# The first norm's x loaded turned for seven of eight feature blocks, and a fourth output block in the opening

## The chip, the cores and the metric

The kernel runs on one core of a Trainium2 chip. The metric is the device time of one execution in microseconds (us), taken as the median of several runs. The engines are named as in the profile: PE (TensorE matmul; PEld its weight loads), DVE (VectorE), ACT (ScalarE), POOL (GpSimd) and SP (SyncE, which issues nearly all DMAs here).

## The reference

The reference is one decoder block in float32 on a sequence of 1024 tokens with 1024 features. Only its beginning is touched by the change:

```python
mod = silu(c) @ w_ada + b_ada                      # 6 x 1024 from the condition c
sh1, sc1, g1, sh2, sc2, g2 = split(mod, 6)
h = rms_norm(x, pre_norm1_w) * (1 + sc1) + sh1     # per token 1/rms, per feature scale and shift
proj = h @ w_in                                    # 1024 x 7696
z, xbc, dt_raw, q, k, v, gates = split(proj)       # gates: two x 1024 columns
...                                                # SSD branch, attention branch, merge, conv-FFN
```

So h = x * rstd[token] * a1[feature] + sh1[feature], with a1 = pre_norm1_w * (1 + sc1).

## The kernel before, in words

Activations are kept turned: features on the 128 partitions, tokens along the row. The 1024 features are eight blocks k = 0..7 (`KD`), the 1024 tokens two halves of 512. Products are in float32 by three passes: every operand is split into a high part (rounded, `hi`) and a rest (`lo`), and hi*hi + hi*lo + lo*hi is accumulated in PSUM, in this kernel 128x128 weights against 512 tokens each.

**The opening.** x lies in memory with tokens as rows. Eight tiles of 128 tokens are loaded (`load_x`), each squared and summed (`square_x` on ACT, `square_v` on DVE), `rstd_x` makes 1/rms (DVE, then a power on POOL), and `scale_x` multiplies each tile by it. For a unit (k, half), `turn_x` has PE transpose four 128x128 pieces into a PSUM bank (L209); `make_h` has ACT make from the bank the high part `hT[k][half]` and the full value `hr` (L215, L216), each as scale a1 and bias sh1; the function that it returns has DVE subtract for the low part (L217). `products(k, half)` then runs nine products on PE: for each of three output blocks (two of `w_xbc`, the first of `w_gate`) hi*hi, lo*hi, hi*lo (L241 to L243). Their weights come in three pieces of feature blocks (`load_first` 0-2, 2-4, 4-8), split by `first_high` (ACT) and `first_low` (DVE). The eight PSUM banks are: `px0` four (two blocks, two halves), `ps_wa` two (gate block 0, two halves), and `ps_wb` and `ps_wc` one each, which take the transposes in turn.

The modulation values of block k come from two 128x1024 tiles of `w_ada1` (shift and scale), loaded by `load_mod(k)` into a ring of eight; `mod_sum` multiplies each by a row silu(c) that is spread over the partitions and sums along the row (DVE, L200), and `mod_end` (DVE, L203, L204) makes sh1 and a1 of that block.

**Behind the opening** come gate blocks 1, 2 and 3: `gate_load`, `gate_split`, and for each half 24 products into a `ps_wa` bank (`gate_half`, L116 to L118), which `gate_out` (ACT, L396) turns into a tanh in `vev` and SP stores. Beside them DVE and ACT make the sums and differences of the quarters of h (`sub`, `hi_of`, `lo_of`, for the operands t2, t1, t3, t4) for what follows: eight passes m = 0..7, each a pair of output blocks computed by Strassen-like seven products (`x_mms(m, p)`, L462 to L464, 12 matmuls each), with the weights' sums (`x_sum`) and splits (`x_split`, `x_ahead` three products ahead) on DVE and ACT. Passes 1 to 3 also hold the remaining modulation sums (`ada_sum`).

The order of the work on PE, DVE, ACT and SP is written out by hand (`tc.manual_schedule`): each engine takes its instructions in the order of the program, and waits on semaphores. A DMA that SP issues has one of eight semaphores and waits until the DMA eight places ahead has landed. Large tiles lie in 43 slots of 4 KB a partition (`Slots`, `SL.get`, `SL.put`).

Of the kernel before, what the change touches and what calls it, by code (L numbers as in the profile page):

```python
# [17 lines left out]
P = 128  # L18
# [44 lines left out]
def kernel(ctx: ExitStack, tc: tile.TileContext, a: dict, out: bass.AP, dbg=None):  # L63
# [82 lines left out]
    A.activation(scl, cT, AF.Silu)  # L146


    hT = [[new_hl(f"hT{k}_{h}") for h in range(2)] for k in range(KD)]
# [3 lines left out]
    junk = SL.get("junk0")  # L153
# [9 lines left out]
    hr = [[[SL.get(f"hr{r}{h}{i}", F32, (P, 2, HALF)) for i in range(2)] for h in range(2)] for r in range(2)]  # L163
    sh1 = const("sh1", [P, KD])
    a1 = const("a1", [P, KD])
    b1c = const("b1c", [P, KD])
    msum = const("msum", [P, KD, 2])

    def load_x(i):
        SP.dma_start(xts[i], a["x"][i * P : (i + 1) * P, :])  # L170

# [19 lines left out]
    n_b = 0  # L191

    def next_bank(name):
        nonlocal n_b
        n_b += 1
        return (ps_wb, ps_wc)[n_b % 2](name)

# [4 lines left out]
    def mod_end(j):  # L202
        V.tensor_tensor(sh1[:, j : j + 1], msum[:, j, 0:1], vec[:, V_B1S + j : V_B1S + j + 1], op=ALU.add)  # L203
        V.scalar_tensor_tensor(a1[:, j : j + 1], msum[:, j, 1:2], b1c[:, j : j + 1], vec[:, V_PN1 + j : V_PN1 + j + 1], op0=ALU.add, op1=ALU.mult)  # L204

    def turn_x(k, half):
        ps = next_bank(f"xtr{k}_{half}")
        for q in range(4):
            T.transpose(ps[:, q * P : (q + 1) * P], xts[4 * half + q][:, k * P : (k + 1) * P], ident)  # L209
        return ps  # L210

    def make_h(k, half, ps):
        xh = hr[k // KH][half][k % KH // 2][:, k % 2, :]
        hi, lo = hT[k][half][:, 0, :], hT[k][half][:, 1, :]
        A.activation(hi, ps, AF.Identity, scale=a1[:, k : k + 1], bias=sh1[:, k : k + 1])  # L215
        A.activation(xh, ps, AF.Identity, scale=a1[:, k : k + 1], bias=sh1[:, k : k + 1])  # L216
# [4 lines left out]
    raw0 = [wp.tile([P, KD, P], F32, tag="wraw", name=f"wf{b}_raw", bufs=3) for b in range(3)]  # L221
    w0 = [[wp.tile([P, KD, P], F32R, tag=f"w{n}", name=f"wf{b}_{n}", bufs=4) for n in ("hi", "lo")] for b in range(3)]
    px0 = [ps_mm("xbc0"), ps_mm("xbc1")]
    pg0 = [ps_wa("gs0_0"), ps_wa("gs0_1")]

# [10 lines left out]
    def products(k, half):  # L236
        for b in range(3):
            o = px0[b][:, half, :] if b < 2 else pg0[half]
            wh, wl = w0[b][0][:, k, :], w0[b][1][:, k, :]
            xh_, xl_ = hT[k][half][:, 0, :], hT[k][half][:, 1, :]  # L240
            T.matmul(o, wh, xh_, start=(k == 0), stop=False)  # L241
            T.matmul(o, wl, xh_, start=False, stop=False)
            T.matmul(o, wh, xl_, start=False, stop=(k == KD - 1))  # L243

    EN = mybir.EngineType
    with tc.manual_schedule(engines={EN.PE, EN.DVE, EN.Activation, EN.SP}):
        for i in range(4):
            load_x(i)
        load_mod(0)
# [3 lines left out]
        load_mod(1)  # L253
        load_first(2, 4)
        load_mod(2)
        load_mod(3)
        load_first(4, 8)
        V.tensor_scalar(b1c, vec[:, V_B1C : V_B1C + KD], 1.0, None, op0=ALU.add)
        for h in range(2):
            pr = next_bank(f"srow{h}")  # L260
# [6 lines left out]
        square_x(3)  # L267
        rstd_x(2)
        scale_x(0, False)
# [5 lines left out]
        mod_end(0)  # L275
        load_mod(4)
        pt0 = turn_x(0, 0)
        for b in range(3):
            first_high(b, 0, 2)
        low = make_h(0, 0, pt0)  # L280
        first_low(0, 0, 2)
        low()
        first_low(1, 0, 2)
        first_low(2, 0, 2)
# [6 lines left out]
        rstd_x(6)  # L291
        scale_x(4, False)
# [3 lines left out]
        pt0 = turn_x(0, 1)  # L296
        mod_sum(1, 0)
        low = make_h(0, 1, pt0)
        mod_sum(1, 1)
        mod_end(1)  # L300
        load_mod(5)
        low()
        mod_sum(2, 0)
        units = [(k, h) for k in range(1, KD) for h in range(2)]
        last = (0, 1)
        for n, u in enumerate(units):
            pt0 = turn_x(*u)
            low = make_h(*u, pt0)
            j = u[0] + 1 + u[1]
            if j < KD:  # L310
                mod_sum(j, 1 - u[1])
                if u[1] == 0:
                    mod_end(j)
                    if j + 4 < KD:
                        load_mod(j + 4)
            low()
            if n in (0, 3):
                for b in range(3):
                    first_high(b, *((2, 4) if n == 0 else (4, 8)))
            if n == 1:  # L320
                for b in range(3):
                    first_low(b, 2, 4)
            elif 3 < n < 7:
                first_low(n - 4, 4, 8)
            products(*last)
            last = u
        products(*last)
        SL.put(junk, *adat, srow, prod, *xts)

# [201 lines left out]
    with tc.manual_schedule(engines={EN.PE, EN.DVE, EN.Activation, EN.SP}):  # L531
# [3 lines left out]
        for n in ("t2", "t1", "t3", "t4"):  # L535
            HX[n] = [new_hl(f"x{n}_{k}") for k in range(KH)]
# [1799 lines left out]
```

## Time and profile before

| what | value |
|---|---|
| median of 3 runs | 1851.14 us (1849.91 to 1851.85) |
| profiled execution | 1848.95 us, its span 1847.1 us |
| PE busy / DVE / ACT in the span | 99% / 70% / 48% |
| first product of the opening | 16.92 us |
| first product of the gate blocks | 65.54 us |
| first product of pass m=0 | 98.18 us |

The span is the time from the first to the last instruction; the profiled execution took 1.85 us more than its span. Times of single instructions are counted from the span's start. A row of the order of time gives start, duration, engine, line, operation, out<-in, and in brackets what the engine was idle for before it.

### The profile page before, as it was taken

What the parts mean: (1) busy time and instruction counts of PE and PEld (TensorE: products, weight loads), DVE (VectorE), ACT (ScalarE), POOL (GpSimd) and SP (SyncE); (2) the same over time, 40 slices, a digit from 0 to 9 for tenths busy, and PEclk for the clock granted to TensorE, in tenths of its full rate; (3) what the DMA queues carried; (4) which work ended last, traced back from release to release, by engine and by line L of the source; (5) the groups of instructions that cost most, each with busy time, mean ns of one, the idle gap of its engine ahead of it and who ended that gap; (6) DMA issues with size and microseconds to landing.
All of it is one profiled execution on the core that took longest, in us unless ns stands there. A gap on an engine that the chain in (4) does not pass through costs nothing.

```text
span 1847.1 us, 24410 instructions
## 1 busy us (share of the span) xinstructions
PE 1822.4 (99%) x8974; PEld 1527.3 (83%) x8974; DVE 1294.9 (70%) x1980; ACT 888.3 (48%) x1720; POOL 144.5 (8%) x128
## 2 busy tenths in 40 slices
PE   6999999999999999999999999999999999999998
PEld 4888899988888888888888888888888888888887
DVE  6777867799654257777667464487898888876545
ACT  6644543456532145565556232565545454455532
POOL 0000000266421000000000100000000000000001
PEclk9999999999999999999999999999999999999999
DMA  8365367687646856566734754122333222378744
GB/s 335 133 216 183 103 208 238 219 315 268 242 125 185 260 132 172 165 170 164 198 104 146 236 196 177 52 95 103 103 120 108 103 97 98 109 235 309 243 158 165
DMA packets 130217, 322.57 MB, mean 175 GB/s; under 512 B 14881, under 2 KB 38833, under 8 KB 130098
## 3 DMA queue, kind: packets, MB, share of 16 engines
q1 hardware_dynamic: 129138, 317.86, 52.3%
q0 software_dynamic: 960, 3.15, 0.5%
q8 instruction: 71, 1.16, 0.3%
q14 instruction: 48, 0.39, 0.1%
HBM read 225.79 MB, written 95.17 MB: 174 GB/s over the span
## 4 chain that ended last, share of the span: by engine, by line
PE 91%; DVE 4%; ACT 3%; issue 1%; DMA 1%; POOL 0%; SPq 0%; DVEq 0%; POOLq 0%; ACTq 0%
PE upx L1744 4%; PE upx L1743 4%; PE upx L1745 4%; PE o L1437 3%; PE dx L2108 2%; PE dx L2107 2%; PE dx L2106 2%; PE upy L1743 2%; PE upy L1744 2%; PE upy L1745 2%; PE v L950 2%; PE z L117 2%; PE z L118 2%; PE z L116 2%; PE dy L2108 2%; PE dy L2107 2%
## 5 line engine op out<-in xcount | busy, mean ns | idle before, releaser
L1743 PE MATMUL upx<-t,wu_t 128*128 128x512 f32 x264 | 103.2, 391 | 0.5 <-DVE cv L2171 0.4
L1744 PE MATMUL upx<-t,wu_t 128*128 128x512 f32 x264 | 102.9, 390 | 0.2 <-DVE t L1861 0.2
L1745 PE MATMUL upx<-t,wu_t 128*128 128x512 f32 x264 | 102.7, 389 | 0.0
L1717 ACT ACTIVATE wu_t<-sab 128x512 fp32r<-128x512 f32 x57 | 34.1, 627 | 128.3 <-DVE sab L1734 128.3
L1425 ACT COPY aT<-at 128x512 f32<-128x512 f32 (+2 forms) x96 | 46.0, 479 | 96.3 <-PE at L1424 96.3
L1437 PEld LDWEIGHTS o<-vt,aT 128*128 128x128 f32 x576 | 75.3, 191 | 9.2 <-ACT aT L1425 4.6
L95 DVE TENSOR_TENSOR g_lo<-gst,g_hi 128x1024 fp32r<-128x1024 f32 (+1 forms) x42 | 47.5, 1135 | 49.0 <-ACT g_hi L94 48.9
L1437 PE MATMUL o<-vt,aT 128*128 128x128 f32 x576 | 80.9, 276 | 0.4 <-ACT aT L1425 0.2
L94 ACT ACTIVATE g_hi<-gst 128x1024 fp32r<-128x1024 f32 (+1 forms) x42 | 41.4, 988 | 63.8 <-DMA gst<-gld_s 35.8
L1398 DVE TENSOR_REDUCE nmx<-sc 128x1 f32<-128x640 f32 (+3 forms) x64 | 65.6, 1025 | 2.2
L1378 PE MATMUL sc<-kst,qst 128*128 128x512 f32 (+2 forms) x192 | 63.8, 340 | 0.0
L1379 PE MATMUL sc<-klo,qst 128*128 128x512 f32 (+2 forms) x192 | 63.3, 346 | 0.0
L1761 DVE SCALAR_TENSOR_TENSOR ug<-cg,vec,ug 128x1023 f32<-128x1023 f32 (+1 forms) x44 | 56.3, 1280 | 6.1 <-ACT ug L1760 5.3
L1743 PEld LDWEIGHTS upx<-t,wu_t 128*128 128x128 f32 x264 | 49.5, 188 | 11.6 <-DVE cv L2171 1.3
L1744 PEld LDWEIGHTS upx<-t,wu_t 128*128 128x128 f32 x264 | 49.6, 188 | 10.6 <-DVE t L1861 0.5
L1745 PEld LDWEIGHTS upx<-t,wu_t 128*128 128x128 f32 x264 | 49.6, 188 | 10.4
L1721 DVE TENSOR_TENSOR wu_t<-sab,wu_t 128x512 fp32r<-128x512 f32 x57 | 39.3, 690 | 26.6 <-ACT wu_t L1717 26.6
L1761 DVE SCALAR_TENSOR_TENSOR uv<-cv,vec,uv 128x1023 f32<-128x1023 f32 (+1 forms) x44 | 56.2, 1278 | 0.9 <-ACT uv L1760 0.9
L1414 DVE RECIPROCAL rsm<-ssum 128x2 f32<-128x2 f32 x64 | 10.6, 166 | 62.4 <-ACT p L1411 35.1
L2227 POOL TENSOR_TENSOR rsf<-rsf,nhalf 128x1 f32<-128x1 f32 x8 | 5.2, 654 | 623.5 <-DVE rsf L2226 623.5
L1416 DVE SCALAR_TENSOR_TENSOR p<-p,coef,p 128x128 f32<-128x128 f32 (+3 forms) x64 | 52.4, 819 | 2.3
L2106 PE MATMUL dx<-wdt_hi,g_hi 128*128 128x512 f32 x132 | 51.3, 389 | 0.0
(537 smaller groups left out, 5923.4 us busy)
## 6 DMA issues: line engine op xcount, KB each, us to landing
adas<-in_w_ada SPq DMA_DIRECT2D x32, 512.0 KB, 5.1
wdr<-in_w_down SPq DMA_DIRECT2D x22, 512.0 KB, 6.2
wtd<-wds SPq DMA_DIRECT2D x22, 512.0 KB, 4.6
wuf<-in_w_up SPq DMA_DIRECT2D x22, 512.0 KB, 3.5
gld_s<-gsum SPq DMA_DIRECT2D x22, 512.0 KB, 2.8
gst<-gld_s SPq DMA_DIRECT2D x20, 512.0 KB, 4.9
wdt_raw<-wtd SPq DMA_DIRECT2D x20, 512.0 KB, 5.1
wuv<-in_w_up SPq DMA_DIRECT2D x19, 512.0 KB, 3.5
```

Source lines behind the costliest of these rows:

```text
L1378: T.matmul(sc[:, n0:n1], qs_[s][:, tsl], ks_[s][:, n0:n1], start=True, stop=False)
L1379: T.matmul(sc[:, n0:n1], qs_[s][:, tsl], kl[s][:, n0:n1], start=False, stop=True)
L1398: V.reduce_max(nmx[:, bq, s : s + 1], sc[:, :L], axis=AX.X, negate=True)
L1416: V.scalar_tensor_tensor(pr[0][:, :L], pr[1][:, :L], coef[:, bq : bq + 1], pr[0][:, :L], op0=ALU.mult, op1=ALU.add)
L1437: T.matmul(po_of[j, grp][:, qi, :], at[:, k, :], vt[j % 2][:, kt, :], start=(kt == 0), stop=(kt == i))
L1743: T.matmul(out_, wh, xh_, start=(k == 0 and first), stop=False, skip_group_check=not first)
L1744: T.matmul(out_, wh, xl_, start=False, stop=False, skip_group_check=not first)
L1745: T.matmul(out_, wl, xh_, start=False, stop=(k == end), skip_group_check=not first)
L1761: V.scalar_tensor_tensor(u[:, d:], c_[:, : S - d], fw[:, 2 - d : 3 - d], u[:, d:], op0=ALU.mult, op1=ALU.add)
L2106: T.matmul(o, gh[:, kk, tsl], wh, start=(k == 0 and not more), stop=False, skip_group_check=more)
L2107: T.matmul(o, gh[:, kk, tsl], wl, start=False, stop=False, skip_group_check=more)
L2108: T.matmul(o, gl[:, kk, tsl], wh, start=False, stop=(k == KF - 1), skip_group_check=more)
```

## The change

1. x is also given turned by the host (`xT`, features as rows). Only feature block 0 is still scaled and transposed on the chip. For k = 1..7 the tile `xT[k]` is loaded, and DVE multiplies it by a1 (per partition) and by a row of rstd that is spread over all partitions (`scale_t`); `make_h` reads that from SBUF and only adds sh1. The 56 other transposes fall away.
2. The row `xrow` is made in two halves: ACT scales the identity by rstd into four diagonal pieces (`diag_of`), one f32 matmul of ones against them (`row_of`) spreads the row, and ACT copies it from PSUM.
3. A fourth output block (the second of `w_gate`) joins the opening: 12 products for each unit, in the banks that the transposes had. It leaves the gate blocks, which are now 2 and 3.
4. `products` runs all blocks' hi*hi, then lo*hi, then hi*lo.
5. The modulation values of block 1 come from PE: 16 matmuls of one column (`mod_mm`), for which the host lays out these two tiles of `w_ada1` the other way. Those of blocks 2 to 7 end on ACT (`mod_end_act`).
6. x's first four tiles are issued right behind `crow`, ahead of the identity, `vec` and `cT`; silu of `cT` moves behind the first squares.
7. Gate block 2 is split ahead of time, with its high part used before its low part (`gate_half_late`); t4's sums, and the loads for `ada_sum`, move into pass m=0.

The diff, cut to its core:

```diff
     cT = const("cT", [P, KD])
-    SP.dma_start(cT, a["cT"])
     ident = const("ident", [P, P])
-    SP.dma_start(ident, a["ident"])
     vec = const("vec", [P, NVEC])
-    SP.dma_start(vec, a["vec"])
...
+    def load_xT(k):
+        SP.dma_start(xT[k].rearrange("p h t -> p (h t)"), a["xT"][k * P : (k + 1) * P, :])
...
+    def mod_mm(j, g, ps):
+        for k in range(KD):
+            T.matmul(ps[:, g : g + 1], adat[(2 * j + g) % NADA][:, k * P : (k + 1) * P], scl[:, k : k + 1], start=(k == 0), stop=(k == KD - 1))
...
+    def mod_end_act(j):
+        A.activation(a1[:, j : j + 1], msum[:, j, 1:2], AF.Identity, scale=vec[:, V_PN1 + j : V_PN1 + j + 1], bias=b1p[:, j : j + 1])
+        A.activation(sh1[:, j : j + 1], msum[:, j, 0:1], AF.Identity, bias=vec[:, V_B1S + j : V_B1S + j + 1])
...
+    def diag_of(half):
+        d = hr[0][1][1][:, half, :]
+        for q in range(4):
+            A.activation(d[:, q * P : (q + 1) * P], ident, AF.Copy, scale=rs1[:, 4 * half + q : 4 * half + q + 1])
+        return d
+
+    def row_of(half, ps):
+        T.matmul(ps, ones, hr[0][1][1][:, half, :], start=True, stop=True)
+
+    def scale_t(k, half):
+        t = xT[k][:, half, :]
+        V.scalar_tensor_tensor(t, t, a1[:, k : k + 1], xrow[:, half, :], op0=ALU.mult, op1=ALU.mult)
...
-    firsts = (("w_xbc", 0), ("w_xbc", 1), ("w_gate", 0))
+    firsts = (("w_xbc", 0), ("w_xbc", 1), ("w_gate", 0), ("w_gate", 1))
...
+    def products(k, half, bs=range(NF), kinds=(0, 1, 2)):
+        for kind in kinds:
+            for b in bs:
+                o = px0[b][:, half, :] if b < 2 else (pg0, pg1)[b - 2][half]
...
+                T.matmul(o, (wh, wl, wh)[kind], (xh_, xh_, xl_)[kind], start=(k == 0 and kind == 0), stop=(k == KD - 1 and kind == 2))
...
         for i in range(4):
             load_x(i)
+        SP.dma_start(ident, a["ident"])
+        SP.dma_start(vec, a["vec"])
+        SP.dma_start(cT, a["cT"])
         load_mod(0)
         load_first(0, 2)
         for i in range(4, 8):
             load_x(i)
         load_mod(1)
+        load_xT(1)
+        load_mod(2)
         load_first(2, 4)
-        load_mod(2)
+        load_xT(2)
         load_mod(3)
+        load_xT(3)
         load_first(4, 8)
...
+        diag_of(0)
+        mod_mm(1, 0, px0[0][:, 1, :])
+        row_of(0, px0[1][:, 1, :])
+        mod_mm(1, 1, px0[0][:, 1, :])
         scale_x(4, False)
         scale_x(5, True)
         scale_x(6, True)
         scale_x(7, False)
...
+        turn_x(1, pt1)
+        mod_end(1, px0[0][:, 1, 0:2])
...
+        A.copy(xrow[:, 0, :], px0[1][:, 1, :])
+        diag_of(1)
+        low01 = make_h(0, 1, pt1)
...
+        scale_t(1, 0)
+        mod_sum(2, 0)
+        products(0, 1, range(3), (0, 1))
...
+        row_of(1, pr)
+        A.copy(xrow[:, 1, :], pr)
+        low01()
+        products(0, 1, range(3), (2,))
+        pg1[1] = ps_wc("gs1_1")
+        products(0, 1, (3,))
...
+        for k in range(2, KD):
+            scale_t(k, 0)
+            scale_t(k, 1)
+            lows = []
+            for h in range(2):
+                lows.append(make_h(k, h))
+                if k == 3:
+                    first_high(2 * h, 4, 8)
+                    first_high(2 * h + 1, 4, 8)
...
+                if k == 4 and h == 0:
+                    for b in range(NF):
+                        first_low(b, 4, 8)
+                if k < KD - 1:
+                    mod_sum(k + 1, h)
...
+                lows[h]()
+                if h == 1 and k < KD - 1:
+                    mod_end_act(k + 1)
+                products(k, h)
...
+        gate_split(3)
         lo_of("t2", 3, r22)
-        pg = gate_half(1, 1)
+        for half in range(2):
+            gate_out(pg1[half], half, gsd[1])
...
         for k in range(KH):
             hi_of("t1", k, r12)
             sub(r11, r22, r11, k)
             lo_of("t1", k, r12)
-        gate_out(pg, 1, gsd[1])
+        pg2.append(gate_half(2, 1))
+        gate_out(pg2[0], 0, gsd[2])
...
+        pg3 = [gate_half(3, 0)]
+        gate_out(pg2[1], 1, gsd[2])
...
+                    if m == 0:
+                        for k in range(KH):
+                            sub(r21, r21, r22, k)
...
+                    if m == 0:
+                        for k in range(KH):
+                            hi_of("t4", k, r21)
...
+                    if m == 0:
+                        for k in range(KH):
+                            lo_of("t4", k, r21)
```

More of the change, by code (lines that the diff above doesn't have):

```diff
@@ L301 @@
+        low01 = make_h(0, 1, pt1)
         load_mod(5)
-        low()
+        load_xT(4)
+        scale_t(1, 0)
         mod_sum(2, 0)
[L304 to L326, printed above, removed]
@@ L327 @@
-        products(*last)
-        SL.put(junk, *adat, srow, prod, *xts)
+        products(0, 1, range(3), (0, 1))
+        pr = ps_wc("xrow1")
+        row_of(1, pr)
[4 more added lines that the diff above has]
+        products(0, 1, (3,))
+        low10 = make_h(1, 0)
+        mod_sum(2, 1)
+        load_mod(6)
+        load_xT(5)
+        scale_t(1, 1)
+        low10()
+        for b in range(NF):
+            first_high(b, 2, 4)
@@ L331 @@
+        gw[2] = w2
+        SL.put(srow, prod, raw3, xrow, *xT[1:])
     order = (("b11", "X"), ("b21", "Z"), ("t2", "X"), ("t1", "Y"), ("t3", "X"), ("b22", "Y"), ("t4", "X"))
```

190 lines of the change are left out of this document (104 added, 86 removed).

## The prediction

> **What bounds the kernel now.** I read the page's busy shares and chain first, then the opening in stretches, then engine by engine.
>
> ```profile
> PE 1822.4 (99%) x8974; PEld 1527.3 (83%) x8974; DVE 1294.9 (70%) x1980; ACT 888.3 (48%) x1720; POOL 144.5 (8%) x128
> ...
> PE 91%; DVE 4%; ACT 3%; issue 1%; DMA 1%; POOL 0%; SPq 0%; DVEq 0%; POOLq 0%; ACTq 0%
> ```
>
> TensorE (PE) is busy in 99% of the span and is 91% of the chain that ended last. So a change in the opening is worth what it does to one moment: when PE enters the Strassen pass m=0 (first `x_mms`), because behind that pass the instructions of every engine stand in the same order in both programs. The stretches (columns: PE, PEld, DVE, ACT, POOL busy, granted clock, DMA share, GB/s):
>
> ```profile
> 15.00:20.00 5.00, 3.18 (x8) 1.90 (x7) 3.76 (x10) 3.89 (x7) 0.00 (x0) 1.00 1.03 419
> 20.00:25.00 5.00, 2.56 (x9) 1.58 (x9) 4.38 (x11) 2.38 (x4) 2.44 (x2) 0.90 1.04 394
> 25.00:30.00 5.00, 4.81 (x13) 3.11 (x12) 4.76 (x12) 3.73 (x7) 0.00 (x0) 0.50 1.04 403
> 35.00:40.00 5.00, 5.00 (x27) 4.04 (x26) 4.67 (x12) 3.94 (x8) 0.00 (x0) 1.00 1.02 402
> 40.00:45.00 5.00, 5.00 (x27) 4.16 (x26) 4.36 (x7) 3.20 (x5) 0.00 (x0) 1.00 0.46 155
> ```
>
> PE waits until about 25 us and is full from 30 us on; DMA is full until 40 us at about 400 GB/s and then eases. PE's own marks, from its order of time:
>
> ```profile
> 16.92 0.80 PE L241 MATMUL xbc<-hT,wf_hi 128*128 128x512 f32 x1 [1.64 <-ACT hT L215]
> ...
> 25.88 0.80 PE L241 MATMUL xbc<-hT,wf_hi 128*128 128x512 f32 x1
> ...
> 33.13 0.60 PE L209 MATMUL xtr<-ident,xt 128*128 128x128 f32 x4
> 33.48 0.47 PE L241 MATMUL xbc<-hT,wf_hi 128*128 128x512 f32 x1
> ...
> 35.99 0.48 PE L241 MATMUL xbc<-hT,wf_hi 128*128 128x512 f32 x1
> ...
> 65.54 0.39 PE L116 MATMUL gs<-hT,wgs_hi 128*128 128x512 f32 x1
> ...
> 98.18 0.39 PE L462 MATMUL xx<-hT,xw_b 128*128 128x512 f32 x1
> ```
>
> At 35.99 the products of feature block k=2 begin, at 65.54 the gate blocks, at 98.18 pass m=0. A unit (one k, one half of the tokens) lasts 35.99 - 33.48 = 2.51 us. The gate blocks are 6 halves of 24 products: (98.18 - 65.54) / 144 = 0.2267 us a product. Nine products are 2.04 us, so the four transposes cost 0.47 us of a unit.
>
> **The change, part by part.** I compare at those three marks and in the pass.
>
> *First mark, start of k=2 (35.99 before).* Durations, taken as the distance from start to start:
>
> ```profile
> 23.57 1.22 DVE L200 SCALAR_TENSOR_TENSOR prod<-adat,srow 128x1024 f32<-128x1024 f32 x1
> 24.72 0.08 DVE L200 DVE_READ_ACCUMULATOR prod<-adat,srow 128x1 f32 x1
> 25.05 0.78 ACT L215 ACTIVATE hT<-xtr,sh,a 128x512 fp32r<-128x512 f32 x1 [0.78 <-PE xtr L209]
> 82.96 2.18 ACT L554 ACTIVATE xt<-hr 128x512 fp32r<-128x512 f32 x4
> 85.03 4.90 DVE L557 TENSOR_TENSOR xt<-hr,xt 128x512 fp32r<-128x512 f32 x8
> 353.40 1.89 PE L1036 MATMUL py<-xd,M 128*128 128x64 f32 x16
> 355.10 0.48 PE L950 MATMUL v<-wv_hi,hT 128*128 128x512 f32 x1
> 5.00 3.78 PE L261 MATMUL srow<-srow,ones 1*128 1x512 f32 x4 [5.00 <-ACT srow L160]
> ```
>
> So a sum over a modulation tile (`mod_sum`) takes 1.15 us of DVE, a 512-wide DVE step 4.90 / 8 = 0.61, a 512-wide ACT step from SBUF 2.18 / 4 = 0.545 and from PSUM 0.7. No one-column matmul is in this trace. The nearest row is L1036: eight f32 matmuls of 64 columns are 16 records, 1.70 us at full clock. I take 1.7 us for each `mod_mm` group of eight; fewer columns could make it about 1 us, half clock 3.4. `row_of` is an f32 matmul of 512 columns, two records; L261 gives 3.78 / 4 = 0.95 each at the slow pace of the first matmuls, so 0.95 for both at full pace and 1.9 at half.
>
> When k=1 can begin is set by loads. From SP's order of time and from the chain in order of time:
>
> ```profile
> 2.50 1.77 SPq L170 DMA_DIRECT2D xt<-in_x  x4
> ...
> 3.84 6.84 DMA xt<-in_x
> ```
>
> The fourth tile of x landed at 3.84 + 6.84 = 10.68. By my count of the new order 8.45 more tiles of 524 KB come in until the first modulation tile of k=1 is there: 4.43 MB, 11.1 us at 400 GB/s. x no longer stands behind three constants (0.24 MB, 0.6 us) and is issued earlier; I take 0.9 us off, so 20.9 (19.9 to 21.8). The first 12 products, started about as much ahead of 16.92, are over by then. From there PE's order is a chain: `mod_mm` 1.7, `row_of` 0.95, `mod_mm` 1.7, the four transposes 0.47, hi on ACT with its hand-over 0.9 (26.6); six products of unit (0,1) 1.36, `row_of` 0.95, ACT's copy and the hi of unit (1,0) with hand-overs 1.4 (30.3), while the last six products of (0,1) run inside that wait; 24 products of k=1 5.44. That is 35.8, 0.2 us before the old mark, though four units with a fourth block are already in it. The rest of the second half's chain runs beside it: in the row below ACT scales x at 22.08, and nothing of that moves behind 25.2, where the `mod_mm` end.
>
> ```profile
> 22.08 2.19 ACT L183 ACTIVATE xt<-xt,rs 128x1024 f32<-128x1024 f32 x2 [1.88 <-POOL rs L143]
> ```
>
> First term: -0.2 us, from -2 (short `mod_mm`) to +3 (half clock, below).
>
> *Second mark, units of k=2 to 7.* Before: 65.54 - 35.99 = 29.55 us. After: 12 units of 12 products, no transposes: 144 x 0.2267 = 32.65. DVE's work for one k is two `scale_t` (0.61 each, at the price of a 512-wide step; the 1024-wide three-operand row halved says the same), two `mod_sum`, two `low`: 1.22 + 2.30 + 1.22 = 4.74 us under PE's 5.44. But DVE reaches k=2 with nothing in hand, spends 0.8 more there on two `first_low`, and in k=4 four 512-wide `first_low` stand ahead of the `low` that PE's third kind of product needs: 4.74 + 2.44 = 7.18, 1.74 over PE's 5.44. About 0.6 is in hand by then, but ACT's four `first_high` in k=3 (4 x 0.545) hold back `mod_end_act(4)` by as much. I charge 1.7 us once; 0 if the lead is larger, 3 if the hand-overs are longer. The loads hide: xT4 is 24.45 tiles (32 us at 400 GB/s) behind the fourth tile of x, so lands near 42, where PE wants k=4 at 35.8 + 10.9 = 46.7 and DVE some 2 us ahead of it; xT7 lands near 51, wanted near 63. If that cover went, every GB/s missing would show here first. Second term: 32.65 + 1.7 - 29.55 = +4.8 (from +3.1 to +6.1).
>
> *Third mark, gate blocks.* Two blocks remain: 4 x 24 x 0.2267 = 21.76 instead of 32.64. What is late next is ACT, whose order decides when a `wa` bank is free:
>
> ```profile
> 68.13 1.20 ACT L554 ACTIVATE xt<-hr 128x512 fp32r<-128x512 f32 x2
> ...
> 72.82 0.63 ACT L554 ACTIVATE xt<-hr 128x512 fp32r<-128x512 f32 x1 [1.29 <-DVE hr L560]
> 73.36 0.58 ACT L396 ACTIVATE vev<-gs 128x512 f32<-128x512 f32 x1
> 73.84 1.05 ACT L94 ACTIVATE wgs_hi<-wgs_raw 128x1024 fp32r<-128x1024 f32 x1
> 74.79 2.18 ACT L554 ACTIVATE xt<-hr 128x512 fp32r<-128x512 f32 x4
> ```
>
> The last `hi_of("t2")` begins 72.82 - 65.54 = 7.3 us after the products end, and DVE's subtractions set that, so it stays. Then come 0.54 for itself, the split of gate 3 (0.95), two `gate_out` (0.5 each), four `hi_of("t1")` (2.18) and the `gate_out` of gate 2's first half (0.6): 12.4 us, where PE has 10.88 us of work. The fourth `ps_wa` bank is the first one again, so gate 3 starts some 1.4 us late (0 to 2.5). Third term: 21.76 + 1.4 - 32.64 = -9.5.
>
> *The pass m=0.* Moved into it are four subtractions and four `lo_of` on DVE (8 x 0.61 = 4.9) and four copies on ACT.
>
> ```profile
> 65.50:98.20 32.70, 32.70 (x146) 27.06 (x146) 23.89 (x37) 17.58 (x31) 0.00 (x0) 1.00 0.29 101
> 98.20:117.30 19.10, 19.10 (x86) 15.83 (x85) 14.38 (x18) 10.40 (x16) 0.00 (x0) 1.00 0.58 206
> ...
> 99.58 0.69 DVE L438 TENSOR_TENSOR xw_t<-xsab,xw_t 128x512 fp32r<-128x512 f32 x1 [4.75 <-ACT xw_t L437]
> ...
> 112.26 0.68 DVE L668 TENSOR_TENSOR xcv<-xx,xevs 128x512 f32<-128x512 f32 x1
> ```
>
> DVE is idle 19.10 - 14.38 = 4.7 us of the pass, 1.4 of it before 99.58 and about 0.7 behind the add at 112.26; 2.6 can take work. The seventh product waits for that add and starts at 98.18 + 72 x 0.2267 = 114.5, so there is 1.6 us of slack: 4.9 - 2.6 - 1.6 = 0.7 late at most. I take +0.4 (0 to 1.5). In the pass behind it DVE is ahead again.
>
> Sum: -0.2 + 4.8 - 9.5 + 0.4 = -4.5 us. The profiled execution took 1848.95 (span 1847.1 and 1.85 around it), which becomes 1844.4; the median of the runs shown is 1851.14, 2.2 above, which becomes 1846.6.
>
> **The clock.** In this kernel PE's clock fell in the opening:
>
> ```profile
> 20.50:23.90 3.40, 1.38 (x5) 0.50 (x4) 2.92 (x6) 1.82 (x2) 2.37 (x2) 1.00 1.05 388
> 23.90:27.30 3.40, 2.79 (x9) 1.67 (x9) 3.16 (x8) 2.62 (x5) 0.00 (x0) 0.51 1.03 412
> 27.30:30.70 3.40, 3.40 (x9) 2.62 (x10) 3.37 (x8) 1.48 (x4) 0.00 (x0) 0.50 1.04 395
> ```
>
> After 3.4 us with 1.38 busy, two stretches of half clock followed. The change puts 16 one-column matmuls there, where before PE stood; my first term takes full clock through them. [...]
>
> **Rivals.**
>
> *No new stalls* (chance 0.25): DVE enters k=2 with a lead and ACT's order is quicker than I read it. Then -0.2 + 3.1 - 10.9 = -8.0: 1843.1. For it: DVE's 4.74 under 5.44. Against: the two sums above, made of steps that stand in the trace.
>
> *Half clock for two stretches* (0.20): it falls near 23.9 as before. The second `mod_mm` group takes 3.4, the transposes 0.9, unit (0,1) and `row_of` twice their time, and full clock returns near 34 to 37. The start of k=2 slips by 4 to 6.5, and the 1.7 of k=4 vanishes because DVE gets its lead. About -4.5 + 3.4 = -1.1: 1850.0.
>
> *Half clock through k=1, slower* (0.10): if the thin stream of one-column matmuls and hand-overs counts as idle again and again, everything from 20.9 to the start of k=2 runs at half: `mod_mm` 6.8, `row_of` 3.8, transposes 0.9, hi 0.9, and 36 products at twice 0.2267 (16.3), some 28.7 us instead of 14.9. Then k=2 starts 13.8 later, less the 1.7 of k=4: -4.5 + 12.1 = +7.6, 1858.7. It decides as soon as full clock returns later than about 43 us. Against it: dense products brought the clock back by 30.7 before.
>
> **How the numbers follow.** My forecast has 0.45. A difference of 0.2%, 3.7 us, is about what a measurement of this kernel can tell from no change. Of the forecast's own range, 1843.5 to 1849.5, about 0.7 lies below 1847.4. Faster: 0.25 + 0.32 = 0.57; same: 0.20 + 0.11 = 0.31; slower: 0.10 and some of the second rival, 0.12. The range 1841.5 to 1852.5 takes in the first three cases with the bounds of `mod_mm` and of the two stalls, and leaves out the last.
>
> **What would show it.** Right: the first product of k=2 at 35 to 37 us, gate 2's first product near 70, pass m=0 near 93.5, a PE wait for DVE's `low` in k=4 and one for ACT's `gate_out` ahead of gate 3, 56 transposes gone. Wrong: a granted clock of 0.5 behind 24 us, PE waiting for DVE in every k, a wait for a load of xT, or a wait of several us at the seventh product of m=0.

## The result, and the profile after

The changed kernel takes 1852.87 us (median of 22 runs, 1850.9 to 1857.7), the kernel before 1850.2 beside it (22 runs, 1848.69 to 1851.85): a ratio of 1.0015, with an interval from 1.0009 to 1.0022. It is 2.7 us slower, where 4.5 us less were forecast. The profiled execution took 1853.68 us (span 1851.8). A second comparison further down gave 1.0010 (1.0001 to 1.0019).

The page of the changed kernel, first the busy time of the engines, then the chain that ended last:

```profile
PE 1823.9 (98%) x8954; PEld 1526.8 (82%) x8954; DVE 1297.5 (70%) x1981; ACT 892.5 (48%) x1744; POOL 143.1 (8%) x128
...
PE 80%; DVE 8%; ACT 4%; DMA 3%; issue 2%; POOL 1%; SPq 0%; DVEq 0%; POOLq 0%; ACTq 0%
```

PE's share of the chain fell from 91% to 80%, so more of the span hangs on DVE, ACT and loads. PE's order of time shows the marks (start in us, duration, what it is, and in brackets the wait):

```profile
15.98 1.22 PE L264 MATMUL xbc<-hT,wf_hi 128*128 128x512 f32 x2 [1.66 <-ACT hT L235]
...
21.31 2.08 PE L202 MATMUL xbc<-scl,adat 128*128 128x1 f32 x16
23.25 1.10 PE L224 MATMUL xbc<-hr,ones 128*128 128x512 f32 x2
24.19 2.64 PE L202 MATMUL xbc<-scl,adat 128*128 128x1 f32 x16
26.69 1.09 PE L214 MATMUL xtr<-ident,xt 128*128 128x128 f32 x4
28.66 1.22 PE L264 MATMUL xbc<-hT,wf_hi 128*128 128x512 f32 x2 [0.87 <-ACT hT L235]
...
39.63 0.61 PE L264 MATMUL xbc<-hT,wf_hi 128*128 128x512 f32 x2
...
54.50 0.72 PE L264 MATMUL xbc<-hT,wf_hi 128*128 128x512 f32 x2 [1.25 <-DVE hT L237]
...
86.81 0.50 PE L116 MATMUL gs<-hT,wgs_hi 128*128 128x512 f32 x1 [1.18 <-ACT vev L474]
```

The products of k=2 begin at 39.63 (35.99 before), 3.6 us later instead of 0.2 earlier. The waits in k=4 (54.50) and ahead of gate block 3 (86.81) are those forecast. The view of stretches (us, then busy time and count of PE, PEld, DVE, ACT, POOL, granted clock, DMA share, GB/s):

```profile
20.00:25.00 5.00, 5.00 (x30) 3.86 (x29) 2.84 (x5) 3.89 (x8) 1.17 (x1) 1.00 1.02 406
25.00:30.00 5.00, 4.13 (x17) 3.55 (x17) 2.94 (x8) 2.60 (x6) 0.00 (x0) 0.50 1.05 396
30.00:35.00 5.00, 5.00 (x16) 3.31 (x16) 2.37 (x4) 2.32 (x5) 0.00 (x0) 0.81 1.04 399
```

PE is shown busy for all of 20 to 25, and then the clock falls to 0.50. In the list of waits these waits of PE are new beside that in k=4 and that ahead of gate 3 (us in total, times, longest):

```profile
PE xx L540 <- DVE xcv L747: 1.2, 1, 1.2
PE dx L2192 <- DVE wdb_lo L95: 0.8, 1, 0.8
PE dx L2192 <- DVE wdt_lo L95: 0.8, 1, 0.8
```

The first is in the Strassen pass m=1, and DVE's order of time shows its cause. The kernel before:

```profile
130.94 1.23 DVE L483 SCALAR_TENSOR_TENSOR prod<-adas,srow 128x1024 f32<-128x1024 f32 x1 [0.75 <-DMA adas<-in_w_ada]
132.09 0.08 DVE L483 DVE_READ_ACCUMULATOR prod<-adas,srow 128x1 f32 x1
132.09 0.69 DVE L668 TENSOR_TENSOR xcv<-xx,xevs 128x512 f32<-128x512 f32 x1
```

The changed kernel:

```profile
133.01 1.23 DVE L561 SCALAR_TENSOR_TENSOR prod<-adas,srow 128x1024 f32<-128x1024 f32 x1 [2.80 <-DMA adas<-in_w_ada]
134.16 0.08 DVE L561 DVE_READ_ACCUMULATOR prod<-adas,srow 128x1 f32 x1
134.16 0.69 DVE L747 TENSOR_TENSOR xcv<-xx,xevs 128x512 f32<-128x512 f32 x1
```

A sum of the second norm waits for its load, and the addition that PE needs stands behind it in DVE's order. It is the fifth sum of the row, and its tile comes from a ring of three (`adas`), so SP can issue its load only when the second sum is done. SP's order of time, before and changed, and DVE's addition for the seventh group of m=0 in the changed kernel:

```profile
123.71 2.67 SPq L477 DMA_DIRECT2D adas<-in_w_ada  x2
```

```profile
125.10 2.67 SPq L555 DMA_DIRECT2D adas<-in_w_ada  x2
113.64 0.69 DVE L747 TENSOR_TENSOR xcv<-xx,xevs 128x512 f32<-128x512 f32 x1
```

Counted from the start of m=0, this addition begins at 15.8 us (14.1 before, where it stood at 112.26), and the load is issued at 27.3 us (25.5 before). So DVE, which got the sums for t4 in the pass m=0, is 1.7 us behind and is still so at the second sum. The change also issues the first three `adas` loads later, behind the third product group of m=0; but the first three sums show no wait for them.

The marks of all profiles, for the sections below (first product; from it to the products of unit (0,1); from there to k=2; from k=2 to the gate blocks; from there to m=0; start of m=0):

| kernel | first | to (0,1) | to k=2 | to gate | to m=0 | m=0 at |
|---|---|---|---|---|---|---|
| before | 16.92 | 8.96 | 10.11 | 29.55 | 32.64 | 98.18 |
| b1_before | 16.71 | 8.95 | 9.96 | 29.53 | 32.64 | 97.79 |
| b2_xt | 17.78 | 8.69 | 10.96 | 29.53 | 32.64 | 99.60 |
| b3_fill | 16.93 | 8.73 | 9.22 | 29.51 | 32.64 | 97.03 |
| after | 15.98 | 12.68 | 10.97 | 34.96 | 23.25 | 97.84 |
| a1_after | 15.19 | 13.20 | 11.78 | 34.82 | 23.28 | 98.27 |
| e1_dve_sum | 16.55 | 10.04 | 10.83 | 35.01 | 23.27 | 95.70 |
| e2_warm | 16.98 | 12.54 | 11.78 | 34.78 | 23.27 | 99.35 |
| e3_adas | 16.46 | 14.08 | 11.60 | 34.99 | 23.26 | 100.39 |
| e4_gate_k4 | 15.46 | 13.21 | 11.88 | 33.71 | 23.17 | 97.43 |
| e5_all | 15.97 | 11.08 | 11.00 | 34.06 | 21.76 | 93.87 |
| e6_all_fill | 15.23 | 9.94 | 9.47 | 34.01 | 21.76 | 90.41 |
| e7_dve_fill | 15.97 | 11.02 | 9.45 | 36.61 | 23.27 | 96.32 |
| e8_all_fill | 15.13 | 10.27 | 9.51 | 34.02 | 21.76 | 90.69 |

### The profile page after: what moved, and what is told of

It is laid out like the page before. It is cut to its first block, busy times and chain, and to the rows that moved or that the text cites. A ratio compares the mean times of both kernels' runs of the same rounds, so it can differ in the third digit from the quotient of the medians.

```text
span 1851.8 us, 24418 instructions
## 1 busy us (share of the span) xinstructions
PE 1823.9 (98%) x8954; PEld 1526.8 (82%) x8954; DVE 1297.5 (70%) x1981; ACT 892.5 (48%) x1744; POOL 143.1 (8%) x128
## 4 chain that ended last, share of the span: by engine, by line
PE 80%; DVE 8%; ACT 4%; DMA 3%; issue 2%; POOL 1%; SPq 0%; DVEq 0%; POOLq 0%; ACTq 0%
PE upx L1829 4%; PE upx L1828 4%; PE upx L1830 4%; PE o L1522 3%; PE upy L1828 2%; PE upy L1829 2%; PE upy L1830 2%; PE v L1035 2%; PE z L117 2%; PE z L118 2%; PE z L116 2%; PE v L1037 2%; DMA gst<-gld_a 2%; PE v L1036 2%; PE at L1509 2%
## 5 line engine op out<-in xcount | busy, mean ns | idle before, releaser
L2192 PE MATMUL dx<-wdt_lo,g_hi 128*128 128x512 f32 x132 | 51.5, 390 | 0.8 <-DVE wdt_lo L95 0.8
```

Of the source, the lines that this page charges most:

```text
L2192: T.matmul(o, gh[:, kk, tsl], wl, start=False, stop=False, skip_group_check=more)
```

## The experiments

Kernels named e are edits of the changed kernel, b of the kernel before.

**e1_dve_sum: block 1's sums back on DVE.**

```
-        mod_mm(1, 0, px0[0][:, 1, :])
         row_of(0, px0[1][:, 1, :])
-        mod_mm(1, 1, px0[0][:, 1, :])
         scale_x(4, False)
         scale_x(5, True)
+        mod_sum(1, 0)
         scale_x(6, True)
         scale_x(7, False)
+        mod_sum(1, 1)
...
-        mod_end(1, px0[0][:, 1, 0:2])
+        mod_end(1, msum[:, 1])
```

> Block 1's two sums are taken by DVE again (two of its 1.22 us sums between the scalings of the second half's x tiles), the sixteen one-column products on PE are gone; all else as in the changed kernel, where the products of k=2 start at 39.63. Theory A, the one-column products stand in PE's order ahead of the four transposes, which wait for nothing else (their last x tile is scaled at 23.9): transposes at about 24.1 instead of 26.69, products of (0,1) at about 25.5 instead of 28.66, k=2 at 36 (between 35 and 37, by how long the half clock lasts), the whole 3 us less than the changed kernel, about 1850. Theory B, only the half clock costs and the order of PE does not matter, since the load of block 1's tiles at 20.9 and the chain behind it set the start: k=2 still at 38.5 to 39.6 and the whole at 1852 to 1853.

Measured: 1849.18 us, 0.9997 of before (0.9988 to 1.0006), so 3.3 us less than the changed kernel by the two ratios. PE's order of time:

```profile
22.55 0.44 PE L214 MATMUL xtr<-ident,xt 128*128 128x128 f32 x2
24.28 0.44 PE L214 MATMUL xtr<-ident,xt 128*128 128x128 f32 x2 [1.29 <-ACT xt L187]
26.59 1.22 PE L264 MATMUL xbc<-hT,wf_hi 128*128 128x512 f32 x2 [1.87 <-ACT hT L235]
```

The transposes start as soon as the scaled x is there, and (0,1) comes 10.04 us behind the first product instead of 12.7 to 14.1; k=2 was somewhat later than expected (37.42, first product 0.57 later). Theory A holds: the one-column products stood in PE's order ahead of transposes that were ready. This is the larger part of the loss at k=2, though not all of it is order: by the granted clock of the stretches the half clock lasts some 3.4 us here (from 25 to 30 us) and 6.8 to 10.2 us in the four profiles of the changed kernel's opening.

**e2_warm: the columns stay, PE is kept busy.** Thirteen f32 products by the row (`dense`) where PE stood idle.

```
+    def dense(n):
+        for _ in range(n):
+            T.matmul(px0[0][:, 1, :], ones, srow[:, :HALF], start=True, stop=True)
...
+        dense(6)
         # transposes 0, 1
+        dense(1)
         # transposes 2, 3
+        dense(2)
...
         products(0, 0)
+        dense(4)
```

> The one-column products stay. PE gets thirteen products of ones by the row (f32, 512 columns, into a bank that is overwritten later) where it stood idle: six ahead of the first transposes (7.1 to 11.9), one between them, two ahead of the first products, four behind those of (0,0). They add nothing to the output. Theory A (PE's order is the cause): the first twelve products may run faster, 2.8 us instead of 5.3, but block 1's tile lands at 20.9 and two groups of columns of 1.9 and 2.5 us and the row's product follow, so the transposes still start at 25.5 to 26.7 and k=2 at 38 to 39.5; the whole 0 to 1.5 us less. Theory B (the half clock is the cause): transposes 0.5 instead of 1.1 us, all products 0.23 us apart, k=2 at 35.5 to 36, the whole 3.5 to 4 us less, about 1849. [...]

Measured: 1853.09 us, 1.0013 (1.0004 to 1.0022). PE's order of time, then stretches:

```profile
7.07 7.45 PE L219 MATMUL xbc<-srow,ones 128*128 128x512 f32 x12
...
20.11 3.59 PE L219 MATMUL xbc<-srow,ones 128*128 128x512 f32 x8
23.54 1.84 PE L202 MATMUL xbc<-scl,adat 128*128 128x1 f32 x16
```

```profile
25.00:27.50 2.50, 2.50 (x19) 2.02 (x18) 0.00 (x0) 1.24 (x5) 0.00 (x0) 1.00 1.06 378
27.50:30.00 2.50, 1.63 (x10) 1.27 (x10) 1.91 (x5) 1.96 (x5) 0.00 (x0) 0.65 1.04 409
30.00:32.50 2.50, 2.50 (x7) 1.93 (x7) 2.10 (x5) 0.14 (x1) 0.00 (x0) 0.50 1.02 401
```

The added products were dearer than reckoned, 7.29 / 6 = 1.21 us each on average at first, where the pace rose on the way, and 3.43 / 4 = 0.86 later, so they delayed what stood behind them (the columns begin at 23.54, not 21.31) and the time of the whole tells nothing of the theories. The clock does: PE ran at full pace from 17.8 us on (the first twelve products took 20.11 - 16.98 = 3.13 us, in the changed kernel 5.33), had no gap from 7.07 to 28.65, and still the clock fell behind the columns (0.65, then 0.50). Neither theory had that.

**e3_adas: the sum out of the way in m=1.**

```
-                if p < {1: 7, 2: 4, 3: 3}.get(m, 0):
+                if p < {1: 7, 2: 5, 3: 3}.get(m, 0) and (m, p) != (1, 4):
                     ada_sum(n_ald < 14)
```

> One of the seven sums over the second norm's weight rows that the pass m=1 takes (the one at the fifth product group, p=4) is moved into the pass m=2. In the changed kernel this sum stood idle 2.80 us for its load (adas), whose first three issues come behind the third group of m=0 there, and the addition that frees the bank for the seventh group stands behind it on DVE: PE waited 1.18 us at 133.7. Theory: the wait of PE for DVE xcv goes wholly, nothing else takes its place, the whole is 1.2 us less. Rival: the addition is then late for another reason (DVE's own pace: it has 0.7 us less work there) and 0.3 us or less is won.

Measured: 1850.96 us, 1.0005 (0.9996 to 1.0014). The wait is gone, and from 118 to 141 us PE's instructions keep a constant distance to those of before (+2.61), where the changed kernel's fall back by 1.5 and a1_after's by 1.1. The theory holds for the mark; the interval of the whole, 3.3 us wide, is too wide for 1.2 us.

**e4_gate_k4: ACT's order at gate 2, DVE's order in k=3 and k=4.**

```
                 if k == 4 and h == 0:
-                    for b in range(NF):
-                        first_low(b, 4, 8)
+                    first_low(3, 4, 8)
...
                 lows[h]()
+                if k == 3:
+                    first_low(2 * h, 4, 8)
+                    if h == 0:
+                        first_low(1, 4, 8)
...
+        gate_out(pg2[0], 0, gsd[2])
         for k in range(KH):
             hi_of("t1", k, r12)
...
         pg2.append(gate_half(2, 1))
-        gate_out(pg2[0], 0, gsd[2])
```

> Two orders changed: the activation that empties gate block 2's first bank stands ahead of the four high parts of t1 on ACT instead of behind them, and the low parts of the opening's four first blocks for k 4 to 7 are spread on DVE, three in k=3 and one in k=4, where the changed kernel had all four in k=4. Theory: the waits of 1.18 us ahead of gate block 3 and of 1.25 us in k=4 both go, pass m=0 starts 2.4 us earlier and the whole is 2.4 us less. Rival for the second: DVE works without a gap from 37.6 on, so the 1.25 us come back in k=3 or k=5 however its pieces are ordered, and only 1.2 us are won. Rival for the first: DVE, full from 84 on, is late with what gate block 3 or pass m=0 needs, and m=0 starts no earlier.

Measured: 1851.18 us, 1.0007 (0.9998 to 1.0016). From k=2 to the gate blocks it took 33.71 us instead of 34.8 to 35.0, so 1.1 to 1.3 won. The wait for the low part in k=4 went wholly, but 24 products took 5.99 us in k=3 and 5.96 in k=4 where PE's own pace is 5.44, so half of what k=4 had lost in the changed kernel (7.60 instead of 5.44, of which the wait is 1.25) stays in smaller pieces: the theory and its rival each had half. The wait ahead of gate 3 went down only to 0.9. PE's wait and ACT's order of time:

```profile
PE gs L116 <- ACT vev L477: 0.9, 1, 0.9
```

```profile
85.53 0.60 ACT L477 ACTIVATE vev<-gs 128x512 f32<-128x512 f32 x1 [1.65 <-DMA gsd<-vev]
```

Moved up, the activation had to wait for the store of the tile that it writes. Neither theory had that.

**e5_all: all four edits**, with the activations of gate block 1 moved up far enough for their stores:

```
             if k > 0:
                 lo_of("t2", k - 1, r22)
+            if k == 1:
+                for half in range(2):
+                    gate_out(pg1[half], half, gsd[1])
```

> Four edits to the changed kernel at once, each with a mark of its own in the trace: block 1's sums on DVE (measured alone: the whole 3.7 us less than the changed kernel), the low parts for k 4 to 7 spread over k=3 and k=4 (measured: the 1.25 us wait gone), the sum of the second norm moved out of the way of the addition in m=1, and for gate block 2 another order: its first bank was still late with the activation moved up, because that waited 1.65 us for the store of the tile (vev) that it writes. So the activations of gate block 1 go up into the idle places of ACT behind the second high part of t2, and their stores are done when gate block 2's first bank is emptied. Theory: the gains add up, since each stands on PE's own path: no wait of PE between k=2 and pass m=0, the whole 1.2 to 2.5 us less than with the first edit alone, 1846 to 1848. Rival: what is gained ahead of m=0 is given back at the first group of m=0 (DVE and ACT are full from 84 on), and the whole stays at 1849.

Measured: 1847.36 us, 0.9984 (0.9975 to 0.9993). Gate 3 no longer waits: 21.76 us from the gate blocks to m=0, exactly 4 x 24 x 0.2267. The gains added up, but not all waits ahead of gate block 2 went: from k=2 to the gate blocks it took 34.06 us, where 144 products at 0.2267 are 32.65, so the smaller pieces that e4_gate_k4 left in k=3 and k=4 are still there. The second half's x tiles were late here: ACT waited 1.41 us for the last, and (0,1) began at 27.05.

**e6_all_fill: the same with repeated products in PE's idle places.**

```
+    def fill(n):
+        for _ in range(n):
+            T.matmul(px0[0][:, 1, :], w0[0][0][:, 0, :], hT[0][0][:, 0, :], start=True, stop=True)
...
-        turn_x(1, pt1)
+        for q in range(4):
+            T.transpose(pt1[:, q * P : (q + 1) * P], xts[4 + q][:, :P], ident)
+            if q == 1:
+                fill(3)
+        fill(5)
```

> As e5_all, and PE repeats eight products that it had made already, into a bank that is overwritten, where it stood idle for 1.3 and 1.9 us: three between the second half's transposes, five behind them. With block 1's sums on DVE the clock fell to 0.57 to 0.74 between 25 and 30 us. Theory (the half clock is priced in products on the path): the granted clock stays 1.00 through 30, the products of (0,1) are 0.23 us apart instead of 0.43, k=2 starts 1.0 to 2.0 us earlier than in e5_all and the whole follows. Rival (the chain of ACT and DVE that makes h of k=1 sets the start of k=2, and slow products only filled its time): the clock stays up, but PE waits for hT instead, and k=2 starts less than 0.5 us earlier.

Measured: 1844.22 us, 0.9969 (0.9958 to 0.9981). Stretches, then PE's order of time:

```profile
25.00:27.50 2.50, 2.33 (x9) 1.61 (x9) 2.50 (x5) 0.79 (x2) 0.00 (x0) 1.00 1.08 390
27.50:30.00 2.50, 2.50 (x11) 1.74 (x10) 1.69 (x4) 2.27 (x5) 0.00 (x0) 1.00 1.02 408
```

```profile
23.05 1.39 PE L219 MATMUL xbc<-hT,wf_hi 128*128 128x512 f32 x5
25.17 0.73 PE L268 MATMUL xbc<-hT,wf_hi 128*128 128x512 f32 x2 [0.73 <-ACT hT L239]
...
34.64 0.61 PE L268 MATMUL xbc<-hT,wf_hi 128*128 128x512 f32 x2
```

The clock stays up and (0,1) to k=2 takes 9.47 us instead of 11.00: 1.5 us are the price of a half clock that lasted some 3.4 us in e5_all. The other 1.9 us by which m=0 starts earlier than in e5_all come from x tiles that landed earlier (0.7 at the first product, 1.1 more at (0,1), where ACT waited 0.75 us for its last tile instead of 1.41), which the edit does not touch.

**b1_before and b2_xt: where do the late waits come from?** b1 has no edit; b2 has only the added input:

```
         "x": np.ascontiguousarray(i["x"])[0],
+        "xT": np.ascontiguousarray(np.ascontiguousarray(i["x"])[0].T),
```

> The kernel before once more, for a second profile of it. The changed kernel and its variants all lost 1.4 to 2.6 us more than the one profile of before between 1640 and 1700 us, in the last MLP product, where PE waits for the low parts of its operands (dx, L2192 there), behind loads of gst; the instructions there are the same. Theory A (chance: those loads land sooner or later in each execution, and the one profile of before was a good one): this profile shows waits of 0.3 us or more there too. Theory B (something in the changed kernel makes them late: the place of a tensor in DRAM, or the slots in SBUF): none here, as before.

> The kernel before with the changed kernel's added input, x turned, lying in DRAM beside the others and not read. Theory B1 (where the tensors lie in DRAM makes the late loads): waits at dx as in the changed kernel, the whole 1 to 2 us above before. Theory B2 (slots in SBUF) or theory A (chance): no difference to before, within 0.1%.

Measured: 1850.65 us (1.0004, 0.9995 to 1.0013) and 1850.71 (the same ratio and interval). PE's waits from 1600 to 1720 us, of b1 and of b2:

```profile
PE dx L2107 <- DVE wdb_lo L95: 0.6, 1, 0.6
```

```profile
PE dx L2107 <- DVE wdt_lo L95: 0.8, 1, 0.8
PE dx L2107 <- DVE wdb_lo L95: 0.5, 1, 0.5
```

The kernel before has them too. From 141 us to the end b1 lost 1.7 us and b2 2.7 against the first profile of before, as the changed kernel did (2.8); a1_after below gained 0.2. So the late waits come and go from execution to execution in both kernels and are not put down to the change, and the added input alone makes no difference that these runs can tell (their interval is 3.3 us wide).

**e7_dve_fill and b3_fill: the repeated products by themselves.** e7 is e1_dve_sum with the `fill` of e6_all_fill; b3 is the kernel before with ten of them:

```
+        fill(4)
         # transposes 0, 1 of the second half
+        fill(3)
         # transposes 2, 3
+        fill(3)
```

> The changed kernel with two edits alone: block 1's sums on DVE, and the eight repeated products in PE's idle places among the second half's transposes. Against the sums on DVE alone (1849.2) this gives the price of the half clock by itself; between the two kernels with all edits the same eight products were worth 3.1 us. Theory (the slow products stand on the path): k=2 starts 19.2 to 19.8 us after the first product instead of 20.9, the whole at 1846.0 to 1847.5. Rival (the 3.1 us came from that pair's other edits or from lucky loads): 1848.5 to 1849.5.

> The kernel before with the same means alone: ten repeated products where PE stood idle between 20.8 and 25.9 us, four behind the products of (0,0), three between the second half's transposes and three behind them. This shows how much of the gain of e6_all_fill belongs to the change and how much any kernel would have had. Theory A (slow products are on the path in the kernel before too): k=2 starts 1.2 to 2 us earlier after the first product (17.0 to 17.8 instead of 18.9 to 19.7) and the whole is at 1848.3 to 1849. Theory B (DVE sets the pace there: it is busy 2.29 to 2.47 of every 2.5 us between 22.5 and 30): less than 0.6 us, 1849.6 to 1850.5.

Measured: e7 1848.64 us, 0.9984 (0.9975 to 0.9993); b3 1848.73 us, 0.9989 (0.9980 to 0.9998). In e7 (0,1) to k=2 takes 9.45 us where e1_dve_sum took 10.83, so 1.4 us, as in the other pair. That k=2 comes 20.5 us behind the first product and not 19.2 to 19.8 lies ahead of (0,1), where ACT waited 1.43 us for the last x tile; by its median alone the rival would stand. The 1.4 us do not reach m=0 in this profile either: k=4 took 9.15 us here and 7.55 in e1_dve_sum, because behind the stall in k=4 the clock fell to 0.50, where it had been 1.00 from 20 to 37.5 us. The stretches of e7:

```profile
50.00:52.50 2.50, 1.26 (x4) 0.93 (x4) 2.50 (x6) 0.01 (x1) 0.00 (x0) 0.84 0.93 374
52.50:55.00 2.50, 2.50 (x7) 1.97 (x6) 2.50 (x4) 1.76 (x4) 0.00 (x0) 0.50 1.03 371
```

From the products of (0,1) to m=0 it is 69.3 us here and 69.1 in e1_dve_sum. In e6_all_fill and e8_all_fill, where the stall in k=4 is smaller, the clock stays up (1.00 from 40 to 60 us in e6_all_fill, products 0.23 us apart behind the stall in e8_all_fill) and the gain reaches m=0 (65.2 and 65.3 us, 66.8 in e5_all). In b3 (0,1) to k=2 takes 9.22 instead of 10.0 to 11.0 us, which lies between the two theories (the median is in theory A's range), and then PE waits for DVE as theory B has it:

```profile
27.02 0.50 PE L243 MATMUL xbc<-hT,wf_hi 128*128 128x512 f32 x1 [0.66 <-DVE hT L217]
```

So some 2 us of what e6_all_fill gains, the kernel before could have had as well (0.4 to 3.7 us by the interval).

**a1_after and e8_all_fill: both once more, side by side.**

> The changed kernel once more, beside e8_all_fill on the same chip, for a second profile. Two things are still told from one profile: the wait of 1.18 us for the addition in m=1 (xcv), which stood in that profile and in that of e4_gate_k4 but in none of e1_dve_sum, e2_warm and e7_dve_fill, whose code there is the same; and the opening, which in e3_adas and e4_gate_k4, the same there, took 25.7 and 25.1 us from the first product to k=2 where the first profile has 23.7. Theory (both go with when loads land and when the clock falls, so they differ from execution to execution): k=2 again 23.5 to 25.7 us after the first product, the wait there or gone, the whole 1851.5 to 1854.

> The kernel of e6_all_fill again, on the same chip as the changed kernel, since six timings are few. Theory: 1844 to 1845.5, at a granted clock of 1.00 throughout the opening, k=2 at 9.4 to 9.6 us behind the first product of (0,1). Rival (the first time it met early loads): 1846 to 1847, by the 1.2 us that its x tiles came earlier than in e5_all and e7_dve_fill.

Measured: a1_after 1851.76 us (1.0010, 1.0001 to 1.0019); e8_all_fill 1844.97 (0.9974, 0.9963 to 0.9985). PE's wait in a1_after:

```profile
PE xx L540 <- DVE xcv L747: 0.8, 1, 0.8
```

PE's wait there stands in three of the six profiles whose code there is the changed kernel's. DVE's wait for the load, its cause, stands in all six, 1.3 to 2.9 us, where the four profiles of the kernel before and of b1, b2 and b3 have 0.5 to 0.75; the smaller ones fit into DVE's slack. k=2 came 25.0 us behind the first product. The changed kernel with its faults mended is thus 0.26% to 0.31% faster than the kernel before, in two comparisons. That includes the repeated products: without them it is 0.16% (e5_all), and by them alone the kernel before becomes 0.11% faster (b3_fill). The x tiles came early in this profile of it too (first product at 15.13), so how much of its gain goes with that is not settled; m=0 at 90.69 is 3.2 us earlier than in e5_all, 1.5 of them from the clock.

## Why the prediction was wrong

Means of the profiles, before (three) and changed (after, a1_after, and e3 and e4 as far as they are the same code):

| step | predicted | measured |
|---|---|---|
| start of k=2 | -0.2 | +4.3 (36.35 to 40.62) |
| k=2 to the gate blocks | +4.8 | +5.4 |
| gate blocks to m=0 | -9.5 | -9.4 |
| m=0 and the pass behind it | +0.4 | +1.4 to +1.9 |
| sum | -4.5 | +1.7 to +2.2; timed +1.9 (1.0010) and +2.7 (1.0015) |

The fourth row is that of the profiles with the wait in m=1. In e1_dve_sum, e2_warm and e7_dve_fill, whose code is the same there, it is +0.4 to +0.8.

- **Start of k=2: the step that failed** is the chain on PE from the landing of block 1's tile, put at 35.8 - 20.9 = 14.9 us at full clock; it took 39.63 - 21.31 = 18.3 in the first profile. The loads ahead of it behaved as forecast (the first product came 1.4 us earlier, the column products began at 20.66 to 22.48 where their load was put at 20.9, and no wait for xT appeared). Two things were wrong in the chain.
  First, full clock through the columns was assumed, which neither profile of the changed kernel shows: the clock fell in the second group, at 25.0 us (at 23.7 in a1_after). That group took 2.50 us instead of 1.7 (3.27 in e3_adas, all of it at a granted 0.50), the transposes and the hand-over behind them 1.97 instead of 1.37, the first six products of (0,1) 2.72 instead of 1.36. These three are 2.8 of the 3.4 us. The prices at full clock were about right: 1.70 to 1.81 us a group (e2_warm, and the first group of e3_adas), 0.94 for the row; fewer columns did not make the group shorter than the 1.70 of the row of 64.
  Second, the chain took the columns' place in PE's order as given, without asking what the transposes behind them had waited for: e1_dve_sum shows that the scaled x was there, and with the sums on DVE (0,1) came 2.6 to 4.0 us earlier behind the first product (1.6 to 3.1 by e5 and e7, whose x landed later). That little could be won by taking 2.3 us off DVE was to be read from the forecast's own working, which charged 3.4 us of PE for them.
- **The half clock** was the rival at 0.20. The fall came, to a granted 0.50 from 25.0 to 31.9 us: the slip from the forecast start is 3.8 us in the first profile and 4.8 in the mean, within or just under its 4 to 6.5. Its relief did not: the stall in k=4 stayed, in the first profile and in a1_after's alike, though k=2 began late. DVE began k=2 late with it, at 37.59 us, as it had waited 2.15 us for the second half's row, whose product stands in PE's order behind the slow ones. From (0,1) to k=2 the filling takes off 1.4 to 1.5 us (e5 to e6, e1 to e7), where the half clock had lasted some 3.4 us; in the changed kernel it lasts 6.8 to 10.2, and its price there was not measured by itself.
- **The fall of the clock.** In the changed kernel the clock fell although PE had no idle place by the trace:

```profile
21.60:25.00 3.40, 3.40 (x26) 2.92 (x26) 1.35 (x2) 2.29 (x4) 1.15 (x1) 1.00 1.02 404
25.00:26.65 1.65, 1.65 (x10) 1.65 (x10) 0.00 (x0) 1.15 (x4) 0.00 (x0) 0.51 1.09 371
```

  Columns included, PE was busy for all of the 3.4 us before the fall here and in e2_warm, and for 3.3 in a1_after. Other falls came with PE idle for part of the time: 1.38 us busy of the 3.4 ahead (the kernel before, 20.5 to 23.9), 0.88 of the 2.45 from 22.55 to 25 (e1_dve_sum, by its rows), 1.26 of 2.50 at the stall in k=4 (e7_dve_fill). And the clock stayed at 1.00 in and behind stretches with 1.78 of 2.50 busy (e7_dve_fill, 25 to 27.5) and 1.60 of 2.50 (e8_all_fill, 22.5 to 25). So the busy time by itself does not tell in these profiles whether the clock falls, and why it falls at the columns is not shown by any run. The transposes of the changed kernel are not the cause there: they begin at 26.69, and the clock had fallen by 25.0 us.
- **k=2 to the gate blocks** was right in kind and near in size: twelve products to a unit at 0.2267, and one stall in k=4 of 7.60 - 5.44 = 2.2 us for 1.7 forecast (bounds 0 to 3).
- **Gate blocks** were right: PE waited 1.18 us for 1.4, at the place and for the reason given (the forecast's own terms add up to 12.6 us and not 12.4, which would have made 1.7 of it). What was missed is that the store of `vev` comes next (e4_gate_k4).
- **Pass m=0** was right about its seventh product (0.36 us later there). What failed was the sentence behind it, that DVE is ahead again in the next pass: DVE is still 1.7 us behind there, counted from the start of m=0, so a load of `adas` is issued that much later. A sum stood 2.4 to 2.9 us for it in three profiles (1.3 to 1.8 in the three others), with an addition behind it for which PE waited 0.8 to 1.2 in those three.

The median of the first comparison lies 0.4 us above the range, since the half clock was taken for one case in five and the load behind the pass was in no case.

## What to carry to other kernels

When work moves from an engine with slack to the one that sets the end, charge its full duration and then ask what in that engine's order stands behind it and was ready. Follow an engine that got more work into the passes behind: what it frees late is loaded late, and what is queued behind the instruction that waits for that load is late too. A price by which a small part is late is best read as a distance between two marks in several profiles: single profiles differed here by 1 to 3 us without a change in the code that made it (b1_before lost 1.7 us and b2_xt 2.7 behind 141 us, and x tiles that landed earlier brought 1.9 us in e6_all_fill).

## What the runs showed of the hardware

- One-column f32 matmuls are not cheap: 1.70 to 1.81 us for eight of them at full pace (e2_warm, and the first group of e3_adas), 3.27 at a granted 0.50 (the second group of e3_adas), and between these where the pace changes inside. The eight of 64 columns in the kernel before took 1.70.
- A granted clock of 1.00 in the view does not show that PE runs at full pace. In b1_before it reads 1.00 where products start 0.43 us apart, 1.9 times the 0.2267 of the later stages. PE's order of time and the stretch:

```profile
28.07 0.63 PE L242 MATMUL xbc<-hT,wf_lo 128*128 128x512 f32 x1
28.50 0.63 PE L243 MATMUL xbc<-hT,wf_hi 128*128 128x512 f32 x1
```

```profile
27.50:30.00 2.50, 2.50 (x7) 1.92 (x7) 2.46 (x7) 1.06 (x4) 0.00 (x0) 1.00 1.07 400
```

  The first twelve products of the changed kernel, from 15.98 to 21.31, are 0.43 us apart at a shown 1.00 too: in that trace the first record of the clock stands at 21.6 us, and the view counts what lies ahead of it as 1.00. So a slow stretch stands there without a record. The distance between equal products tells the pace.
- Repeating eight products that were already made, in places where PE stood idle, delayed nothing that these profiles show and took 1.4 to 1.5 us off the way from (0,1) to k=2. In e7_dve_fill a fall of the clock to 0.50 in k=4 took it back.
- Why the changed kernel's times spread wider (1850.35 to 1857.7 over both comparisons, the kernel before 1848.3 to 1852.3 over all) was not tried. Its way to k=2 differs by up to 2 us between profiles (23.7 to 25.7 us from the first product), with how long the half clock lasts.
